# Sums of squares over heads: one plain float32 product, or two float32r products of squares that GpSimd splits

## The chip, the core and the metric

The kernel runs on one core of one Trainium2 chip. A core has a matrix engine, TensorE (PE in the profile; PEld is its loading of stationary operands), a vector engine, VectorE (DVE), a scalar engine, ScalarE (ACT), and GpSimd (POOL); SyncE (SP) issues transfers. Each engine works through its own queue in order, and the engines wait for each other by semaphores. The metric is the device time of one execution in microseconds; lower is better.

## What is computed

A two-layer model over 512 tokens of width 1024, all in float32. Layer 0 mixes tokens with stick-breaking attention and with a gated recurrence of 4 heads (`hgrn2`), layer 1 with sliding-window attention of 16 query heads and 4 key heads of width 64. Each layer then has a gated feed-forward part and a gated embedding. The part that matters here is the normalisation over the width of a head:

```python
def rmsnorm(x, g):
    xf = x.astype(jnp.float32)
    y = xf * lax.rsqrt(jnp.mean(xf * xf, axis=-1, keepdims=True) + EPS)
    return (y * g.astype(jnp.float32)).astype(x.dtype)
...
    o_b = rmsnorm(o_b.astype(h.dtype), hg_norm) * jax.nn.silu(gb.reshape(B, S, HG_HEADS, HG_DV))
...
    q = rmsnorm(q.reshape(B, S, SW_HEADS, SW_DIM), q_norm)
    k = rmsnorm(k.reshape(B, S, SW_KV_HEADS, SW_DIM), k_norm)
```

The first is taken over 4 heads of width 128 (layer 0), the other two over 16 and 4 heads of width 64 (layer 1).

## The kernel before

Activations lie feature by token: a tile has 128 features in its partitions and the 512 tokens along its rows. A large product is computed from split operands: weights and activations are each stored as a high and a low part in float32r, and three float32r products (high by high, high by low, low by high: lines 185 to 187, `mm3`) stand for one float32 product. Where no split was made, the kernel issues one plain float32 product.

A sum over the features of a head runs across partitions, so it is a product with a constant matrix. In `hg_head` (layer 0, run for each of the 4 heads) the head's output `pso` is squared by ScalarE (line 509, `osq`), a plain float32 product with a matrix of ones sums it (line 511, `pn`), ScalarE takes the logarithm and the exponential of the sum (`act`, line 71), and VectorE multiplies (line 515, `ob`). In `mixer_c` (layer 1) `project` squares each tile of two heads (line 729, `sqc`), and `normed` sums it by a plain product with a matrix that holds two blocks of ones (line 735, `pn`). That happens ten times: for two tiles of keys, and for eight tiles of queries, of which the first two come together and the other six one by one in the loop over `jt`, two rounds ahead of their use. So there are 14 such sums.

Around the four sums of layer 0 TensorE has the products of the stick-breaking attention's values (line 593, `poa`), the dense products (`psfm`) and the score products of the next head (`psd`, `psl`). Around the ten of layer 1 it has dense products, the products `pstm` of the values, and the attention's `pl`, `pt` and `poc`. `sp` is the pool of the statistics; its tag `sq` has two buffers.

The order on each engine is made by a scheduler when the program is built: it walks through the code's operations with its own estimate of their lengths and picks what it takes to be ready. The program that comes out has a fixed order on each engine. GpSimd has little to do before the change: constants at the start, small memsets, a few transfers.

Of the kernel before, what the change touches and what calls it, by code (L numbers as in the profile page):

```python
# [9 lines left out]
F32 = mybir.dt.float32  # L10
F32R = mybir.dt.float32r
U8 = mybir.dt.uint8
AF = mybir.ActivationFunctionType
ALU = mybir.AluOpType

P = 128
T = 512
# [8 lines left out]
SET_EL = "natural_log_exp_and_others"  # L26
# [24 lines left out]
class Kern:  # L51
# [34 lines left out]
    def bank(self, name, tag="mm"):  # L86

        if self.turn is None:
            return self.ps.tile([P, T], F32, tag=tag, name=name)
        i = self.turn % 8  # L90
        self.turn += 1
        if i % 2:
            return self.ps.tile([P, T], F32, tag="hg" if i % 4 == 3 else "mm", name=name)
        if i % 4 == 0:
            self.pair = self.zpair(name)
        return self.pair[:, i % 4 // 2, :]

    def setup(self):
        nc, A = self.nc, self.A
        self.cp = self.pool("const")  # L100
        self.hp = self.pool("hpool")
        self.xa = self.pool("xa", 16)
        self.wp = self.pool("wpool", 7)
        self.sp = self.pool("stat", 1)
        self.ps = self.pool("psum", 2, psum=True)
        self.turn = None
        cp = self.cp

        self.gains = cp.tile([P, V_CONV + 48], F32, name="gains")[:, 0:V_CONV]
        nc.scalar.dma_start(out=self.gains, in_=A["vecs"][:, 0:V_CONV])  # L110
        self.h = [self.hp.tile([P, T], F32, name=f"h{m}") for m in range(KT)]
        self.early = []
        for m in range(KT):
            nc.sync.dma_start(out=self.h[m], in_=A["xT"][m * P:(m + 1) * P, :])
            if m in EARLY:
                raw = self.wp.tile([P, 1024], F32, tag="wraw", name="wraw", bufs=2)
                for c in (slice(0, 512), slice(512, 1024)):
                    nc.sync.dma_start(out=raw[:, c], in_=A["w_ab"][EARLY[m]][:, c])
                self.early.append(raw)
        self.vec = cp.tile([P, NV - V_CONV], F32, name="vec")  # L120
        nc.gpsimd.dma_start(out=self.vec, in_=A["vecs"][:, V_CONV:])
        self.ones = cp.tile([P, P], F32, name="ones")
        nc.vector.memset(self.ones, 1.0)

        warm = self.bank("warm", "hg")
        for _ in range(WARM):
            nc.tensor.matmul(warm[:, 0:P], self.ones, self.ones, start=True, stop=True)
        self.eps = cp.tile([P, 1], F32, name="eps")
        nc.vector.memset(self.eps, EPS)
        self.rcol = cp.tile([P, NT], F32, name="rcol")  # L130
        self.one = cp.tile([P, 1], F32, name="one")
        nc.vector.memset(self.one, 1.0)
        self.cst = cp.tile([P, 3 * P], F32, name="cst")
        nc.gpsimd.dma_start(out=self.cst, in_=A["cst"][:, 0:3 * P])
        self.ident = self.cst[:, 0:P]
        self.flip = self.cst[:, P:2 * P]
        self.flips = self.cst[:, 0:2 * P]
        self.blk = self.cst[:, 2 * P:3 * P]
        self.cstr = cp.tile([P, 4 * P], F32R, name="cstr")
        self.ntri = self.cstr[:, 0:P]  # L140
        self.nones = self.cstr[:, P:2 * P]
        self.negm = self.cstr[:, 2 * P:3 * P]
        self.identr = self.cstr[:, 3 * P:4 * P]

    def matrices(self, tmp):
        nc = self.nc
        nc.gpsimd.dma_start(out=tmp[:, :3 * P], in_=self.A["cst"][:, 3 * P:6 * P])
        nc.gpsimd.tensor_copy(out=self.cstr[:, 0:3 * P], in_=tmp[:, 0:3 * P])
        nc.gpsimd.tensor_copy(out=self.cstr[:, 3 * P:4 * P], in_=self.ident)

    def v(self, c):
        if c < V_CONV:
# [86 lines left out]
    def square(self, m, st):  # L239
        nc = self.nc  # L240
        h = self.h[m]
        if m == 0:
            st["acc"] = self.sp.tile([P, T], F32, tag="acc", name="acc")
            nc.scalar.activation(st["acc"], h, AF.Square)
            return
        sq = self.sp.tile([P, T], F32, tag="sq", name="sq", bufs=2)
        nc.scalar.activation(sq, h, AF.Square)
        nc.vector.tensor_tensor(out=st["acc"], in0=st["acc"], in1=sq, op=ALU.add)
        if m == KT - 1:
            st["ss"] = [self.sp.tile([P, T], F32R, tag="sq", name=n, bufs=2) for n in ("sqhi", "sqlo")]  # L250
            nc.scalar.copy(out=st["ss"][0], in_=st["acc"])
            nc.vector.tensor_tensor(out=st["ss"][1], in0=st["acc"], in1=st["ss"][0], op=ALU.subtract)

    def norm(self, st, tag="mm"):

        nc = self.nc
        ps = self.bank("psn", tag)
        for i in range(2):
            nc.tensor.matmul(ps, self.nones, st["ss"][i], start=(i == 0), stop=(i == 1))
        r = self.sp.tile([P, T], F32, tag="rstd", name="rstd")  # L260
        self.act(SET_EL, r, ps, AF.Ln, scale=-1.0 / DM, bias=self.eps)
        self.act(SET_EL, r, r, AF.Exp, scale=-0.5)
        st["rstd"] = r
# [30 lines left out]
    def mixer_ab(self, st):  # L294
        nc, A = self.nc, self.A
        W = A["w_ab"]
        with ExitStack() as ctx:
# [3 lines left out]
            cp = self.pool("ab_const", 1, ctx=ctx)  # L301
# [89 lines left out]
            def hg_head(hd, q, k, p64):  # L391
# [11 lines left out]
                for b in range(NT):  # L403
# [3 lines left out]
                                        in1=self.flips.unsqueeze(1).broadcast_to([P, 2, 2 * P]), op=ALU.mult)  # L407

                ps = None
                for li in range(7):  # L410
# [8 lines left out]
                    n = T // (2 * c)  # L419
# [29 lines left out]
                    else:  # L449
                        for r in range(2):  # L450
                            h = slice(r * 64, r * 64 + 64)
                            nc.scalar.copy(out=ad.rearrange("p (j r) t -> p j r t", j=2)[h, :, r, 64:128],
                                           in_=po.rearrange("p (j r t) -> p j r t", j=2, r=2)[h, :, r, :])
# [47 lines left out]
                for j in range(NT):  # L501
                    nc.tensor.matmul(ps[:, j * P:(j + 1) * P], ib[j][:, vs], ad[:, j, :], start=first, stop=False, skip_group_check=True)
                    first = False
                    if j in off:
                        o = off[j]
                        nc.tensor.matmul(ps[:, (j + 1) * P:T], ib[j][:, vs], ao[:, o[0] * P:(o[-1] + 1) * P],
                                         start=False, stop=False, skip_group_check=True)
                sq = tp.tile([P, T], F32, tag="fp", name="osq", bufs=2)
                nc.scalar.activation(sq, ps, AF.Square)
                pn = bank("hg", "pn")  # L510
                nc.tensor.matmul(pn, self.ones, sq, start=True, stop=True)
                self.act(SET_EL, sq, pn, AF.Ln, scale=1.0 / P, bias=self.eps)
                self.act(SET_EL, sq, sq, AF.Exp, scale=-0.5)
                o = kp.tile([P, T], F32, tag="ob", name="ob")
                nc.vector.scalar_tensor_tensor(out=o, in0=ps, scalar=self.v(V_HGN), in1=sq, op0=ALU.mult, op1=ALU.mult)
# [123 lines left out]
            for i in range(4):  # L639
                d = dense(i + 1)  # L640
                h, s = hg_head(i, *heads[i]), sb_pair(i, *pairs[i])
                for c in PLAN if i < 3 else LAST:
                    next({"h": h, "s": s, "d": d}[c], None)
                for _ in d:
                    pass
# [55 lines left out]
    def mixer_c(self, st, bias, fill):  # L701
        nc, A = self.nc, self.A
        xs = st["xs"]
        W = A["w_c"]
        with ExitStack() as ctx:
# [26 lines left out]
            def normed(y, sq, gain, tag, bufs):  # L732

                pn = self.bank("pn")
                nc.tensor.matmul(pn, self.blk, sq, start=True, stop=True)  # L735
                self.act(SET_EL, sq, pn, AF.Ln, scale=1.0 / 64, bias=self.eps)
                self.act(SET_EL, sq, sq, AF.Exp, scale=-0.5)
                o = kp.tile([P, T], F32, tag=tag, name=tag, bufs=bufs)
                nc.vector.scalar_tensor_tensor(out=o, in0=y, scalar=gain, in1=sq, op0=ALU.mult, op1=ALU.mult)
                return o  # L740

            kn = [project(8 + i) for i in range(2)]
            kn = [normed(*x, self.v(V_KN), "kn", 2) for x in kn]
            vt = []
            for _ in tok:
# [78 lines left out]
            for jt in range(2):  # L824
                qs[jt] = normed(*two[jt], gq, "qn", 3)
            for jt in range(8):
                for n0 in (0, 2):
                    pend.append(scores(jt, n0))
                    if jt + 2 < 8:
                        if n0 == 0:  # L830
                            nxt = project(jt + 2)
                        else:
                            qs[jt + 2] = normed(*nxt, gq, "qn", 3)
                    if len(pend) > 2:
                        values(*pend.pop(0))
# [217 lines left out]
```

## Time and profile before

| | |
|---|---|
| time, median of 3 runs | 1327.49 us (1326.45 to 1328.64) |
| the profiled execution, its time | 1326.3 us |
| the profiled execution, its span | 1324.5 us |
| PE busy | 1309.1 us, 99% of the span |
| DVE busy | 863.1 us, 65% |
| ACT busy | 684.0 us, 52% |
| POOL busy | 18.7 us, 1% |
| granted clock of TensorE, mean | 0.999 |

The time holds the span of the profiled instructions and 1.8 us around it. In a row of the timeline the first number is the start in microseconds from the span's start, the second the duration; then come engine, line, operation, output and inputs, and shape; a row merges neighbours of one form and gives their count, and ends with the idle time before it and what ended that. A plain float32 product stands in the trace as two instructions, a float32r product as one. Ends of matrix products are modelled, so the start-to-start distance tells more than a duration.

### The profile page before, as it was taken

To read this page: it belongs to the slowest core of one execution; us is meant where nothing else is said; L and a number is where in the kernel's file an instruction comes from. 1 tells how busy PE (TensorE), PEld (TensorE's weight loads), DVE (VectorE), ACT (ScalarE), POOL (GpSimd) and SP (SyncE) were. 2 spreads that over 40 slices of the span, in tenths; PEclk is the share of its full clock that TensorE was granted. 3 is DMA by queue.
4 is the path that set the end of the run, shared out by engine and by line. 5 is a ranking of instruction groups with operands and counts; after the bars stand their busy time and mean duration, and the time that the engine had idled before them with its cause. 6 is when DMAs were issued, how large, how long until landed. Compare 5 with 4: busy or idle time off the path is not lost.

```text
span 1324.5 us, 16856 instructions
## 1 busy us (share of the span) xinstructions
PE 1309.1 (99%) x6162; PEld 1055.2 (80%) x6162; DVE 863.1 (65%) x1609; ACT 684.0 (52%) x1224; POOL 18.7 (1%) x108
## 2 busy tenths in 40 slices
PE   9999999999999999999999999999999999999998
PEld 7787767788888888888888866678888888888887
DVE  6567876766677347776558387755777536776555
ACT  6566876845345224444465466654544324455341
POOL 2000000000000000000000000000000000000000
PEclk9999999999999999999999999999999999999999
DMA  6321211134553333323333211122332333332332
GB/s 208 108 64 49 59 39 47 48 98 116 90 142 98 106 102 101 99 91 94 107 112 91 85 48 32 33 82 94 102 102 89 94 107 96 96 96 88 90 109 80
DMA packets 38821, 118.96 MB, mean 90 GB/s; under 512 B 4433, under 2 KB 10881, under 8 KB 38737
## 3 DMA queue, kind: packets, MB, share of 16 engines
q1 hardware_dynamic: 38032, 116.41, 29.5%
q0 software_dynamic: 560, 1.45, 0.5%
q8 instruction: 48, 0.79, 0.2%
q14 instruction: 37, 0.30, 0.1%
q10 hardware_dynamic: 144, 0.02, 0.0%
HBM read 115.37 MB, written 2.49 MB: 89 GB/s over the span
## 4 chain that ended last, share of the span: by engine, by line
PE 93%; DVE 4%; ACT 2%; issue 1%; DMA 0%; SPq 0%; DVEq 0%; ACTq 0%
PE psfm L185 25%; PE psfm L187 25%; PE psfm L186 25%; PE pl L765 2%; PE poc L817 2%; PE pstm L220 1%; PE pstm L218 1%; PE pstm L219 1%; PE pt L800 1%; PE poa L593 1%; ACT sl L71 1%; PE psz L576 1%; PE pn L735 1%; PE psl L443 1%; PE pspp L185 1%; PE pspp L187 1%
## 5 line engine op out<-in xcount | busy, mean ns | idle before, releaser
L185 PE MATMUL psfm<-xhi,whi 128*128 128x512 f32 (+1 forms) x1200 | 470.8, 393 | 1.3 <-ACT xhi L235 1.3
L170 ACT CAST whi<-wraw 128x512 fp32r<-128x512 f32 (+1 forms) x428 | 260.0, 613 | 406.2 <-PE psfm L186 319.9
L186 PE MATMUL psfm<-xlo,whi 128*128 128x512 f32 (+1 forms) x1200 | 467.0, 389 | 0.8 <-DVE xlo L236 0.7
L187 PE MATMUL psfm<-xhi,wlo 128*128 128x512 f32 (+1 forms) x1200 | 467.5, 390 | 0.1
L171 DVE TENSOR_TENSOR wlo<-wraw,whi 128x512 fp32r<-128x512 f32 (+1 forms) x428 | 287.9, 677 | 170.4 <-ACT whi L170 149.5
L185 PEld LDWEIGHTS psfm<-xhi,whi 128*128 128x128 f32 x1200 | 226.0, 188 | 49.3 <-issue 2.0
L186 PEld LDWEIGHTS psfm<-xlo,whi 128*128 128x128 f32 x1200 | 225.8, 188 | 48.8 <-DVE xlo L236 2.3
L187 PEld LDWEIGHTS psfm<-xhi,wlo 128*128 128x128 f32 x1200 | 225.5, 188 | 47.6 <-issue 1.3
L185 PE MATMUL psfm<-ghi,whi 128*128 128x512 f32 x352 | 136.9, 389 | 0.0
L186 PE MATMUL psfm<-glo,whi 128*128 128x512 f32 x352 | 136.9, 389 | 0.0
L187 PE MATMUL psfm<-ghi,wlo 128*128 128x512 f32 x352 | 136.9, 389 | 0.0
L858 DVE TENSOR_TENSOR u<-psfm,rstd 128x512 f32<-128x512 f32 x88 | 60.7, 691 | 64.0 <-PE psfm L187 60.4
L861 ACT ACTIVATE cy<-u,vec 128x512 f32<-128x512 f32 x88 | 71.7, 817 | 43.8 <-DVE u L858 43.8
L862 DVE SCALAR_TENSOR_TENSOR cy<-u,vec,cy 128x512 f32<-128x512 f32 x88 | 66.1, 752 | 39.0 <-ACT cy L861 38.9
L185 PEld LDWEIGHTS psfm<-ghi,whi 128*128 128x128 f32 x352 | 66.1, 188 | 13.7
L187 PEld LDWEIGHTS psfm<-ghi,wlo 128*128 128x128 f32 x352 | 66.1, 188 | 13.7
L186 PEld LDWEIGHTS psfm<-glo,whi 128*128 128x128 f32 x352 | 66.1, 188 | 13.7
L291 DVE TENSOR_TENSOR h<-h,psfm 128x512 f32<-128x512 f32 x48 | 33.0, 688 | 57.3 <-PE psfm L187 57.3
L863 DVE SCALAR_TENSOR_TENSOR cy<-u,vec,cy 128x512 f32<-128x512 f32 x88 | 65.9, 751 | 2.7
L875 ACT CAST ghi<-cy 128x512 fp32r<-128x512 f32 x44 | 27.4, 623 | 49.4 <-DVE cy L872 49.4
L236 DVE SCALAR_TENSOR_TENSOR xlo<-h,gains,xhi 128x512 fp32r<-128x512 f32 x48 | 36.5, 761 | 7.0 <-ACT xhi L235 6.6
L235 ACT ACTIVATE xhi<-h,gains 128x512 fp32r<-128x512 f32 x48 | 34.6, 724 | 11.0 <-DVE h L291 6.8
(216 smaller groups left out, 1303.3 us busy)
## 6 DMA issues: line engine op xcount, KB each, us to landing
wraw<-w_up SPq DMA_DIRECT2D x88, 512.0 KB, 3.5
wraw<-w_dn SPq DMA_DIRECT2D x32, 512.0 KB, 3.5
wraw<-w_ab SPq DMA_DIRECT2D x18, 512.0 KB, 3.5
wraw<-w_pg SPq DMA_DIRECT2D x16, 512.0 KB, 3.5
wraw<-w_dn SPq DMA_DIRECT2D x32, 192.0 KB, 2.3
wraw<-w_c SPq DMA_DIRECT2D x10, 512.0 KB, 3.4
wraw<-w_abo SPq DMA_DIRECT2D x8, 512.0 KB, 3.6
wraw<-w_co SPq DMA_DIRECT2D x8, 512.0 KB, 3.5
```

The lines of the kernel that those rows point to most:

```text
L170: nc.scalar.copy(out=hi[:, :d1 - d0], in_=r)
L171: nc.vector.tensor_tensor(out=lo[:, :d1 - d0], in0=r, in1=hi[:, :d1 - d0], op=ALU.subtract)
L185: t.matmul(ps, w[0], x[0], start=first, stop=False)
L186: t.matmul(ps, w[0], x[1], start=False, stop=False)
L187: t.matmul(ps, w[1], x[0], start=False, stop=last)
L235: nc.scalar.activation(hi, h, AF.Identity, scale=g)
L236: nc.vector.scalar_tensor_tensor(out=lo, in0=h, scalar=g, in1=hi, op0=ALU.mult, op1=ALU.subtract)
L291: self.nc.vector.tensor_tensor(out=self.h[m], in0=self.h[m], in1=ps, op=ALU.add)
L858: nc.vector.tensor_tensor(out=u[:, 2:], in0=ps, in1=rstd, op=ALU.mult)
L861: nc.scalar.activation(y, u[:, 2:], AF.Identity, scale=w[2], bias=w[3])
L862: nc.vector.scalar_tensor_tensor(out=y, in0=u[:, 1:T + 1], scalar=w[1], in1=y, op0=ALU.mult, op1=ALU.add)
L863: nc.vector.scalar_tensor_tensor(out=y, in0=u[:, 0:T], scalar=w[0], in1=y, op0=ALU.mult, op1=ALU.add)
```

## The change

A new helper `sums` splits the squares on GpSimd into a high part (a cast to float32r) and a low part (square minus high part), and sums them by two float32r products into the same bank. Both sites call it. The matrix of ones of layer 0 becomes the existing `nones`, which holds minus ones, so the sign of the scale turns; the block matrix `blk` moves to the constants that are stored as float32r, and the transfers and casts of the constants are cut differently (256 and 512 columns, before 384 and 384).

```diff
-        self.cst = cp.tile([P, 3 * P], F32, name="cst")
-        nc.gpsimd.dma_start(out=self.cst, in_=A["cst"][:, 0:3 * P])
+        self.cst = cp.tile([P, 2 * P], F32, name="cst")
+        nc.gpsimd.dma_start(out=self.cst, in_=A["cst"][:, 0:2 * P])
...
-        self.blk = self.cst[:, 2 * P:3 * P]
-        self.cstr = cp.tile([P, 4 * P], F32R, name="cstr")
...
+        self.cstr = cp.tile([P, 5 * P], F32R, name="cstr")
+        self.blk = self.cstr[:, 0:P]
...
-        nc.gpsimd.dma_start(out=tmp[:, :3 * P], in_=self.A["cst"][:, 3 * P:6 * P])
-        nc.gpsimd.tensor_copy(out=self.cstr[:, 0:3 * P], in_=tmp[:, 0:3 * P])
-        nc.gpsimd.tensor_copy(out=self.cstr[:, 3 * P:4 * P], in_=self.ident)
+        nc.gpsimd.dma_start(out=tmp, in_=self.A["cst"][:, 2 * P:6 * P])
+        nc.gpsimd.tensor_copy(out=self.cstr[:, 0:4 * P], in_=tmp)
+        nc.gpsimd.tensor_copy(out=self.cstr[:, 4 * P:5 * P], in_=self.ident)
...
+    def sums(self, pn, by, sq):
+
+        nc = self.nc
+        ss = [self.sp.tile([P, T], F32R, tag="sq", name=n, bufs=2) for n in ("sqhi", "sqlo")]
+        nc.gpsimd.tensor_copy(out=ss[0], in_=sq)
+        nc.gpsimd.tensor_tensor(out=ss[1], in0=sq, in1=ss[0], op=ALU.subtract)
+        for i in range(2):
+            nc.tensor.matmul(pn, by, ss[i], start=(i == 0), stop=(i == 1))
...
-                nc.tensor.matmul(pn, self.ones, sq, start=True, stop=True)
-                self.act(SET_EL, sq, pn, AF.Ln, scale=1.0 / P, bias=self.eps)
+                self.sums(pn, self.nones, sq)
+                self.act(SET_EL, sq, pn, AF.Ln, scale=-1.0 / P, bias=self.eps)
...
-                nc.tensor.matmul(pn, self.blk, sq, start=True, stop=True)
+                self.sums(pn, self.blk, sq)
```

Nine lines are added ahead of `norm`, so a line behind them has a number that is 9 higher in the changed kernel.

On GpSimd the queue after the constants (`cstr`, `hgm`) changes as follows, first before, then now; `u` is a tile of the feed-forward part:

```order
L149 CAST cstr<-cst 128x128
L148 CAST cstr<-cstt 128x384
L312 CAST hgm<-mf 128x3x128 x4
L857 MEMSET u 128x2 x2
L674 DMA bias<-relb 32x16
```

```order
L149 CAST cstr<-cst 128x128
L148 CAST cstr<-cstt 128x512
L321 CAST hgm<-mf 128x3x128 x4
L258 CAST sqhi<-osq 128x512
L259 ISA
L259 TENSOR_TENSOR sqlo<-osq,sqhi 128x512
L258 CAST sqhi<-osq 128x512
L259 TENSOR_TENSOR sqlo<-osq,sqhi 128x512
```

A cast and a subtraction for each of the four heads now stand between the constants and the memsets (ten more pairs stand in layer 1), and ahead of the first subtraction the program has an instruction `ISA` that it names a reload of GpSimd's library.

On TensorE, the end of the second head of layer 0, where `pso` is that head's output; the third head is alike, before and then now:

```order
L502 MATMUL pso<-ad,ib 128x128
L593 MATMUL poa<-sl,va 64x128 x2
L593 MATMUL poa<-sl,va 64x256
L511 MATMUL pn<-osq,ones 128x512
L593 MATMUL poa<-sl,va 64x256
L593 MATMUL poa<-sl,va 64x384 x2
L593 MATMUL poa<-sl,va 64x512 x2
L405 MATMUL psd<-qh,kk 128x128
```

```order
L511 MATMUL pso<-ad,ib 128x128
L602 MATMUL poa<-sl,va 64x128 x2
L602 MATMUL poa<-sl,va 64x256 x2
L602 MATMUL poa<-sl,va 64x384
L261 MATMUL pn<-sqhi,cstr 128x512
L602 MATMUL poa<-sl,va 64x384
L602 MATMUL poa<-sl,va 64x512
L261 MATMUL pn<-sqlo,cstr 128x512
L602 MATMUL poa<-sl,va 64x512
```

The first product of the sum moved behind two more value products, the second stands two value products later, and the score product `psd` comes after four dense products. In the first head the second product stands much further back: 18 dense products and a block of score products `psz` lie between the last value product and it, and `psd` comes after it.

On TensorE, where the first two query tiles of layer 1 are normalised, before and then now:

```order
L187 MATMUL psfm<-xhi,wlo 128x512
L735 MATMUL pn<-sqc,cst 128x512 x2
L185 MATMUL psfm<-xhi,whi 128x512
L186 MATMUL psfm<-xlo,whi 128x512
L187 MATMUL psfm<-xhi,wlo 128x512
```

```order
L187 MATMUL psfm<-xhi,wlo 128x512
L261 MATMUL pn<-sqhi,cstr 128x512
L261 MATMUL pn<-sqlo,cstr 128x512
L261 MATMUL pn<-sqhi,cstr 128x512
L185 MATMUL psfm<-xhi,whi 128x512
L186 MATMUL psfm<-xlo,whi 128x512
L261 MATMUL pn<-sqlo,cstr 128x512
L774 MATMUL pl<-kn,qn 128x128 x2
```

Between the second tile's two products stand two dense ones. On ScalarE the logarithm of the first tile's sum now stands ahead of the second tile's square, where it stood behind it. At the other sums the two products stand as follows: fourth head of layer 0, high part behind two dense products and one more of them between; key tiles, the four products of the two tiles spread among 256-column products `pstm`, four ahead of the first and then three, two and three between them; third query tile, high part behind all of `pl`, one dense product between; the next three query tiles, high part ahead of the last three `poc`, low part behind them; the last two, both where the plain product stood.

## Rows read from the trace of the kernel before

**Rows 1.** The page, busy time, share and instructions of each engine.

```profile
PE 1309.1 (99%) x6162; PEld 1055.2 (80%) x6162; DVE 863.1 (65%) x1609; ACT 684.0 (52%) x1224; POOL 18.7 (1%) x108
```

**Rows 2.** Timeline of PE in dense float32r products, first and last of a run of 30.

```profile
900.09 0.39 PE L186 MATMUL psfm<-xlo,whi 128*128 128x512 f32 x1
...
906.66 0.39 PE L185 MATMUL psfm<-xhi,whi 128*128 128x512 f32 x1
```

**Rows 3.** Timeline around the sums of the two key tiles, PE and ACT.

```profile
736.54 1.17 ACT L729 ACTIVATE sqc<-y 128x512 f32<-128x512 f32 x2 [0.82 <-DVE y L727]
...
737.79 1.96 PE L735 MATMUL pn<-sqc,cst 128*128 128x512 f32 x4
...
739.83 0.29 PE L220 MATMUL pstm<-whi,xlo 128*128 128x256 f32 x1
...
741.02 0.28 PE L218 MATMUL pstm<-whi,xhi 128*128 128x256 f32 x1
```

**Rows 4.** Timeline of POOL at the start.

```profile
7.13 0.29 POOL L149 CAST cstr<-cst 128x128 fp32r<-128x128 f32 x1 [3.07 <-DMA cst<-cst]
8.00 0.51 POOL L148 CAST cstr<-cstt 128x384 fp32r<-128x384 f32 x1 [0.57 <-DMA cstt<-cst]
9.17 3.57 POOL L312 CAST hgm<-mf 128x384 uint8<-128x384 f32 x4 [0.66 <-DMA mf<-hgm]
```

**Rows 5.** One line's instructions (minimum, median, maximum ns; first and last start).

```profile
L248 DVE TENSOR_TENSOR acc<-acc,sq x42: 677/684/991, 9.6 to 1277.3; 128x512 f32<-128x512 f32 x42
```

**Rows 6.** Transfers by line: count, KB each, median us from issue to landing.

```profile
mf<-hgm POOLq DMA_DIRECT2D x2, 192.0 KB, 6.2
```

**Rows 7.** Timeline at the end of layer 0's second head, PE and ACT.

```profile
167.25 0.60 ACT L509 ACTIVATE osq<-pso 128x512 f32<-128x512 f32 x1 [1.16 <-PE pso L502]
167.94 1.12 PE L511 MATMUL pn<-osq,ones 128*128 128x512 f32 x2
169.00 2.15 PE L593 MATMUL poa<-sl,va 128*64 128x256 f32 x10
...
171.08 0.49 PE L405 MATMUL psd<-qh,kk 128*128 128x128 f32 x2
```

**Rows 8.** Timeline at the end of layer 0's fourth head, PE and ACT.

```profile
254.87 0.60 ACT L509 ACTIVATE osq<-pso 128x512 f32<-128x512 f32 x1
...
255.60 1.05 PE L511 MATMUL pn<-osq,ones 128*128 128x512 f32 x2
...
257.20 0.39 PE L186 MATMUL psfm<-xlo,whi 128*128 128x512 f32 x1
```

**Rows 9.** Timeline around the sums of the first two query tiles, PE and ACT.

```profile
751.74 0.63 ACT L729 ACTIVATE sqc<-y 128x512 f32<-128x512 f32 x1 [0.33 <-DVE y L727]
...
756.25 1.02 PE L735 MATMUL pn<-sqc,cst 128*128 128x512 f32 x2
...
757.77 0.67 ACT L71 ACTIVATE sqc<-pn,eps 128x512 f32<-128x512 f32 x1
757.92 1.12 PE L735 MATMUL pn<-sqc,cst 128*128 128x512 f32 x2 [0.65 <-ACT sqc L729]
...
759.35 0.40 PE L187 MATMUL psfm<-xhi,wlo 128*128 128x512 f32 x1
```

**Rows 10.** Timeline at the third query tile's sum, PE.

```profile
767.93 1.12 PE L735 MATMUL pn<-sqc,cst 128*128 128x512 f32 x2 [0.61 <-ACT sqc L729]
...
769.95 0.39 PE L186 MATMUL psfm<-xlo,whi 128*128 128x512 f32 x1
```

**Rows 11.** Timeline at the last query tile's sum, PE and ACT.

```profile
833.88 0.64 ACT L729 ACTIVATE sqc<-y 128x512 f32<-128x512 f32 x1
...
836.39 1.12 PE L735 MATMUL pn<-sqc,cst 128*128 128x512 f32 x2
...
837.36 1.04 PE L800 MATMUL pt<-cst,lg 128*128 128x128 f32 x8
```

**Rows 12.** Who waited for whom, window of layer 0's heads (us in total, times, longest).

```profile
PE psl L443 <- DVE ad L445: 5.2, 3, 1.7
```

More of the change, by code (lines that the diff above doesn't have):

```diff
@@ L137, in setup @@
         self.flips = self.cst[:, 0:2 * P]
-        self.blk = self.cst[:, 2 * P:3 * P]
-        self.cstr = cp.tile([P, 4 * P], F32R, name="cstr")
[L140 to L143, printed above, removed]
+        self.cstr = cp.tile([P, 5 * P], F32R, name="cstr")
+        self.blk = self.cstr[:, 0:P]
+        self.ntri = self.cstr[:, P:2 * P]
+        self.nones = self.cstr[:, 2 * P:3 * P]
+        self.negm = self.cstr[:, 3 * P:4 * P]
+        self.identr = self.cstr[:, 4 * P:5 * P]
     def matrices(self, tmp):
         nc = self.nc
-        nc.gpsimd.dma_start(out=tmp[:, :3 * P], in_=self.A["cst"][:, 3 * P:6 * P])
-        nc.gpsimd.tensor_copy(out=self.cstr[:, 0:3 * P], in_=tmp[:, 0:3 * P])
-        nc.gpsimd.tensor_copy(out=self.cstr[:, 3 * P:4 * P], in_=self.ident)
+        nc.gpsimd.dma_start(out=tmp, in_=self.A["cst"][:, 2 * P:6 * P])
+        nc.gpsimd.tensor_copy(out=self.cstr[:, 0:4 * P], in_=tmp)
+        nc.gpsimd.tensor_copy(out=self.cstr[:, 4 * P:5 * P], in_=self.ident)
     def v(self, c):
```

## The prediction, made before the changed kernel ran

> **What bounds the kernel now.** I first read the busy shares: TensorE is busy for 1309.1 of 1324.5 us, VectorE 65%, ScalarE 52%, GpSimd 1% [rows 1]. So a microsecond that TensorE is spared is worth up to a microsecond, and one that it stands still costs one; there are only 15.4 us of idle time to win. Then I read the timelines at the 14 sums for two things: how far TensorE's next start is moved by a sum, and how long the square had been ready when TensorE came to it. For the second the reader looks for the end of the square on ScalarE and the start of `pn` on TensorE: where the two lie 0.1 us apart, as in layer 0 [rows 7], any later delivery shows up in the time; where `pn` starts 1.9 us after the square [rows 11], there is cover.
>
> **What the change takes away.** Thirty dense float32r products start (906.66 - 900.09)/29 = 0.227 us apart [rows 2]. The plain float32 pair of the key tiles starts at 737.79; the products behind it are (741.02 - 739.83)/10 = 0.119 us apart, and the third of them starts at 739.83, so the pair took 739.83 - 0.24 - 737.79 = 1.80 us, 0.90 each [rows 3]. Two float32r products cost 0.45 instead of 0.90, and 14 sums save 14 x 0.45 = 6.3 us of TensorE's time. That is all that the change can give directly.
>
> **What it adds.** Each square now passes through two GpSimd instructions before TensorE can finish the sum. The cast: 128 columns took 0.29 us and 384 took 0.51 [rows 4], so 0.86 ns a column and 0.18 us fixed, 0.62 us for 512. The subtraction reads two operands, and no such instruction of GpSimd is in this trace. Its lower bound is the cast's 0.62 us. For the upper bound I take the slowest cast there is: four of 384 columns took 3.57 us beside VectorE's work, 0.89 each [rows 4], less 0.18 fixed 1.85 ns a column, and for two operands of 512 columns 0.18 + 1024 x 0.00185 = 2.07 us. I take 1.24 us, two plain casts, since the plain cast to the same type is the nearest row; 0.62 and 2.07 stay as ends. A handover costs about 0.1 us (square ends 167.85, `pn` starts 167.94 [rows 7]). So the high part can be multiplied 0.1 + 0.62 + 0.1 = 0.82 us after the square, the low part 0.82 + 1.24 + 0.1 = 2.16 us after it. [...]
>
> **The sum, site by site**, against the work that TensorE had done at the same point before. S is the end of the square.
>
> Second and third head of layer 0 [rows 7]: S = 167.85. The value products `poa` come in pairs that fill half the array each and overlap: ten instructions with 2048 columns took 169.00 to 171.08, 1.02 ns a column. TensorE, which came to the plain product at 167.94, now has 640 more columns ahead of the sum, 0.65 us, to 168.59; the high part is ready at 168.67 and done at 168.90; 896 columns follow, with their broken pair about 1.1 us, to 170.0; the low part is ready at 170.01, done 170.24; the last 512 columns, alone, 0.91: 171.15 against 171.08. Cost 0.1 each: the saving is eaten by one more broken pair and the wait.
>
> First head, in the same clock: high part done 168.90, all 1408 columns behind it (1.6 us) to 170.5 instead of 171.08, the low part 0.23 later: -0.3. Its low part waits for the library reload, whose price no row shows: at least nothing, at most about the slowest transfer that GpSimd issues, 6.2 us [rows 6]. The low part is ready at 170.0 plus the reload, and TensorE comes to it after 18 dense products, 170.5 + 4.1 = 174.6, and a score block that I don't count: 4.6 us or more are hidden, so the reload costs 0 to 1.6 us; I take 0. [...]
>
> Fourth head [rows 8]: S = 255.47. Two dense products more, then a wait for the high part until 256.29; one dense product; the low part is ready at 257.63, done 257.86, against 257.20 before: +0.7.
>
> Key tiles [rows 3]: the two squares end at 737.71 (736.54 + 1.17) and, one square of 0.63 us behind the start, at 737.17. Four 256-column products, high part to 738.50, three more to 738.86, then a wait for the low part until 739.33. GpSimd takes the second cast only now (739.33 to 739.95): its high part at 740.05, its low part at 741.39, done 741.62, against 741.02: +0.6.
>
> First two query tiles [rows 9]: the first square ended at 752.37, so its parts are there when TensorE comes at 756.25; both are done at 756.70. ScalarE's logarithm of it, 0.67 us, now stands ahead of the second square: that one ends at 757.47 + 0.63 = 758.10. Its high part follows at 758.92, two dense products to 759.60, its low part at 760.26, done 760.49, against 759.35: +1.1. Here TensorE stands still about 2.9 us, for 0.65 before, and nothing else is queued ahead that could fill it.
>
> Third query tile [rows 10]: S = 767.88; high part 768.70, one dense product, low part 770.04, done 770.27, against 769.95: +0.3.
>
> Last five query tiles, one shown [rows 11]: S = 834.52, the plain product started at 836.39 and held TensorE for 0.97 us. The low part is ready at 836.68, the high part's product (with the switch from one kind of product to the other about 0.3) is done then, and the next product starts at 836.96 instead of 837.36: -0.4. In three of the five the parts stand apart and pay one switch more: -0.35 on average, -1.75 for the five.
>
> The larger transfer of constants (512 columns for 384) and its longer cast, 0.11 us, lie in the first 9 us, long before a sum of squares is taken: nothing. GpSimd's memsets and transfers behind the splits start later than 258 us and wait for others anyway: nothing.
>
> Sum: -0.3 + 2 x 0.1 + 0.7 + 0.6 + 1.1 + 0.3 - 1.75 = **+0.9 us**. Of the 6.3 us saved nearly all goes into waiting. Against the profiled execution that is 1326.3 + 0.9 = 1327.2; the median of the runs lies 1.2 us above that execution, so 1328.4 us on the scale of medians.
>
> **How far it can move.** With a subtraction of 0.62 us the waits shrink at six sites, and the same walk gives -2.4 us. With 2.07 us it gives about +10: each sum but the first then waits, two of them twice, because the second tile's cast stands behind the first tile's subtraction.
>
> **The rivals.** *All waits hidden*: TensorE gains the full 6.3 us, 1321.2 us. For it speaks that the order was made so that the products come when their parts are due by the scheduler's estimate; against it that the gaps left for a subtraction are often one to three products, 0.2 to 0.7 us, less than even a cast takes. It also needs the stall of 5.2 us in three places at the score products [rows 12] to go away or stay as it is.
>
> *GpSimd is held up beside VectorE*: slower, 1337.5 us at the upper end. During the four casts at 9.2 to 12.7 us VectorE's additions took up to 0.99 us, for a median of 0.68 [rows 4, 5]: each slowed the other. A weight split of VectorE falls beside nearly every split of squares in layer 1. It decides from a subtraction (with its waiting) of about 1.4 us on: each 0.1 us more costs about 1 us over all sites, and 0.9 + 1.8 us is what can be measured.
> [...]
>
> *The reload or the late start of the next head*: a reload above 6 us, or the first head's `psd` five microseconds later than before, so that score products wait for VectorE more than the 5.2 us of now [rows 12]: 3 to 6 us, about 1332.5.
>
> *The products are not cheaper* can be left at 2%: float32r products of this very kind cost 0.227 us [rows 2].
>
> **How the numbers follow.** Forecast (waits eat the gain): 0.45. All or most waits hidden: 0.18. GpSimd held up: 0.22. Reload or next head: 0.13. The rest 0.02. A measurement of this kernel can tell about 0.2%, 2.7 us. Of the forecast 0.41 lies within that, 0.03 above and 0.01 below; both slow cases (0.35) lie above; of the fast case 0.17 lies below and 0.01 within; the rest is halved between same and slower. That makes 0.18 faster, 0.43 same, 0.39 slower. The range reaches from 1322.5, which leaves most of the full gain out, to 1337, near the upper end of the held-up GpSimd.
>
> **What would show it.** TensorE's idle time in the window of the heads and in layer 1's attention up by about 6 us in all, with "GpSimd `sqlo`" as what ended it; two float32r `pn` products at 0.2 to 0.3 us each; a subtraction near 1.24 us; the largest new waits at the first two query tiles (about 2.9 us) and at the key tiles. Wrong would make it a subtraction under 0.7 us or over 1.6 us, a stall of several microseconds at the first low part, or new waits at `psl`.

## The result, and where the time went

The changed kernel takes **1336.1 us** (six runs, 1334.5 to 1337.4) against 1327.3 (six runs, 1326.5 to 1328.6): a ratio of 1.0065, 95% interval 1.0054 to 1.0075, so 8.8 us **slower**. That lies within the range, but not in the forecast, which was no measurable change. The profiled execution has a span of 1334.8 us, 10.3 above that of before. The page of after, to be held against [rows 1], and TensorE's longest waits by tile:

```profile
PE 1310.8 (98%) x6162; PEld 1057.8 (79%) x6162; DVE 864.5 (65%) x1609; ACT 682.6 (51%) x1224; POOL 47.7 (4%) x136
```

```profile
PE psl L452 <- DVE ad L454: 5.2, 4, 1.7
PE pn L261 <- POOL sqhi L258: 3.8, 4, 2.1
PE pn L261 <- POOL sqlo L259: 3.3, 6, 0.9
PE psl L452 <- ACT l L71: 2.2, 2, 1.6
PE psfm L185 <- ACT xhi L235: 1.8, 1, 1.8
```

(Line numbers behind 253 are nine higher than before; L258 is the cast, L259 the subtraction, L261 the product.) TensorE was to be busy 6.3 us less and is busy 1.7 us *more*: its products became cheaper and something else in its busy time dearer. Its idle time went from 15.4 to 24.0 us. Where, is read by cutting both timelines at four instructions that every version has: the first `pstm` product (about 22 us), VectorE's first `u` of layer 0's feed-forward (about 318), the first `pstm` of layer 1's attention, the first `u` of layer 1's feed-forward. All versions run here, cut in the same way (one profiled execution each; the medians stand beside). One execution of q1plain and one of direct ran in a slower state, and the ratios leave them out.

| us | start | layer 0's heads | between | attention | rest | median of runs |
|---|---|---|---|---|---|---|
| before | 21.85 | 295.53 | 413.40 | 197.64 | 396.08 | 1327.3 |
| **after** | 23.43 | 300.26 | 413.40 | 201.66 | 396.05 | 1336.1 |
| const | 23.15 | 295.55 | 413.41 | 197.56 | 396.03 | 1327.4 |
| heads | 23.31 | 300.35 | 413.37 | 197.59 | 396.08 | 1331.8 |
| attn | 21.17 | 295.48 | 413.45 | 201.46 | 396.04 | 1330.9 |
| tail | 22.02 | 295.50 | 413.40 | 201.25 | 396.03 | 1328.7 |
| q1plain | 23.10 | 300.23 | 413.38 | 200.61 | 396.08 | 1335.1 |
| fill | 22.20 | 300.45 | 413.38 | 197.33 | 396.04 | 1330.9 |
| nolow | 23.78 | 294.22 | 413.41 | 189.98 | 396.11 | 1318.5 |
| idle | 21.41 | 295.50 | 413.43 | 198.30 | 396.06 | 1327.9 |
| vsplit | 22.23 | 299.85 | 413.40 | 201.96 | 396.06 | 1335.7 |
| direct | 22.16 | 292.98 | 413.40 | 189.11 | 396.05 | 1316.4 |
| mix3 | 21.94 | 295.51 | 413.44 | 196.66 | 396.05 | 1325.0 |
| mix2 | 21.83 | 295.56 | 413.38 | 196.54 | 396.09 | 1326.2 |

The heads lost 4.73 us and the attention 4.02, together 8.75, close to the 8.8 of the medians. The 1.6 us of the start are not the change's: with the same constants the start takes 21.2 to 23.8 us.

**GpSimd's instructions are as long as forecast.** Minimum, median and maximum of one instruction in ns, and the first split in time:

```profile
L258 POOL CAST sqhi<-sqc x10: 609/660/1129, 743.5 to 846.0; 128x512 fp32r<-128x512 f32 x10
L259 POOL TENSOR_TENSOR sqlo<-sqc,sqhi x10: 1262/1282/1631, 744.2 to 847.2; 128x512 fp32r<-128x512 f32 x10
```

```profile
123.77 0.61 POOL L258 CAST sqhi<-osq 128x512 fp32r<-128x512 f32 x1 [111.07 <-ACT osq L518]
124.47 1.27 POOL L259 TENSOR_TENSOR sqlo<-osq,sqhi 128x512 fp32r<-128x512 f32 x1
```

Forecast were 0.62 and 1.24 us. The first subtraction of the program starts 0.09 us behind its cast: no cost of a reload is to be seen. Three instructions that ran beside VectorE's were longer, and TensorE waited for the low parts behind them:

```profile
261.38 1.59 POOL L259 TENSOR_TENSOR sqlo<-osq,sqhi 128x512 fp32r<-128x512 f32 x1
745.60 0.95 POOL L258 CAST sqhi<-sqc 128x512 fp32r<-128x512 f32 x1
766.29 1.63 POOL L259 TENSOR_TENSOR sqlo<-sqc,sqhi 128x512 fp32r<-128x512 f32 x1
```

Against 1.27 and 0.61 us these are 0.32, 0.34 and 0.36 us more, some 1.0 us of the 8.8.

**Heads.** TensorE at the second head's sum, against [rows 7] and the start of the block before (first row):

```profile
167.15 0.86 PE L593 MATMUL poa<-sl,va 128*64 128x128 f32 x6
...
168.73 1.51 PE L602 MATMUL poa<-sl,va 128*64 128x128 f32 x10
170.53 0.50 PE L261 MATMUL pn<-sqhi,cstr 128*128 128x512 f32 x1 [0.29 <-POOL sqhi L258]
170.97 1.08 PE L602 MATMUL poa<-sl,va 128*64 128x384 f32 x4
171.97 0.49 PE L261 MATMUL pn<-sqlo,cstr 128*128 128x512 f32 x1
172.40 1.07 PE L602 MATMUL poa<-sl,va 128*64 128x512 f32 x2
173.40 0.50 PE L185 MATMUL psfm<-xhi,whi 128*128 128x512 f32 x1
...
185.30 0.68 PE L452 MATMUL psl<-e 128*128 128x128 f32 x4 [0.85 <-DVE ad L454]
```

From the first value product to the end of the block it is 173.40 - 168.73 = 4.67 us; before, 171.08 - 167.15 = 3.93. Between half-width value products a full product takes 0.43 us, not 0.23 (170.53 to 170.97): the two take 0.86 us, the plain one 1.06 (167.94 to 169.00), so a sum saves only 0.2 us here. The wait for the high part adds 0.3. The rest, the 16 value products themselves, takes 3.5 us instead of 2.9: the sum now breaks their pairs in two places instead of one. The last 512 columns, left alone, take 1.00 us (172.40 to 173.40), where 2048 columns took 2.08 before [rows 7]. Then a score product of the next head waits 0.85 us for VectorE; its counterpart before didn't wait. The third head repeats it (+0.43 and 0.85); the fourth lost 1.1 at its sum (a wait of 0.94 for `sqlo`, 0.32 of it by the longer subtraction above); the first gained 0.2. All waits at `psl` grew from 5.8 to 7.9 us. Some 0.5 us of the 4.73 I can't place.

**Attention.** TensorE at the first two query tiles, against [rows 9], and its granted clock there (stretch, length, busy time of PE, PEld, DVE, ACT, POOL, then the clock):

```profile
763.56 0.39 PE L261 MATMUL pn<-sqhi,cstr 128*128 128x512 f32 x1
763.79 0.39 PE L261 MATMUL pn<-sqlo,cstr 128*128 128x512 f32 x1
766.26 0.50 PE L261 MATMUL pn<-sqhi,cstr 128*128 128x512 f32 x1 [2.09 <-POOL sqhi L258]
...
767.97 0.79 PE L261 MATMUL pn<-sqlo,cstr 128*128 128x512 f32 x1 [0.75 <-POOL sqlo L259]
768.69 1.66 PE L774 MATMUL pl<-kn,qn 64*128 64x128 f32 x8
770.28 0.79 PE L187 MATMUL psfm<-xhi,wlo 128*128 128x512 f32 x1
770.87 0.63 PE L185 MATMUL psfm<-xhi,whi 128*128 128x512 f32 x1
771.30 0.63 PE L186 MATMUL psfm<-xlo,whi 128*128 128x512 f32 x1
```

```profile
766.00:768.00 2.00, 0.99 (x4) 0.52 (x4) 0.75 (x1) 0.00 (x0) 1.84 (x2) 0.96 0.00 0
768.00:774.00 6.00, 6.00 (x18) 4.14 (x19) 2.43 (x11) 1.32 (x2) 0.00 (x0) 0.50 0.01 3
774.00:776.00 2.00, 2.00 (x9) 1.59 (x8) 0.69 (x1) 1.48 (x6) 0.00 (x0) 0.83 0.00 0
```

TensorE stands still 2.09 + 0.75 us, as forecast. What was not: behind it the granted clock is 0.50 from 767.9 to 774.7 us, and dense products start 0.43 us apart instead of 0.227. That costs half of 6.8, 3.4 us, and shows as busy time. Before, the same stretch had 1.00. The other executions agree: the mean granted clock is 0.993 to 0.996 in the six of the changed kernel, and 0.996 to 0.999 in those of the kernel before. The last query tile, against [rows 11], is the gain that was meant:

```profile
834.29 0.50 PE L261 MATMUL pn<-sqhi,cstr 128*128 128x512 f32 x1
834.63 0.42 PE L261 MATMUL pn<-sqlo,cstr 128*128 128x512 f32 x1
834.88 1.04 PE L809 MATMUL pt<-cst,lg 128*128 128x128 f32 x8
```

0.59 us instead of 0.97. From the first to the last transpose `pt`, five sums, after needs 89.92 us, before 91.61.

### The profile page after: what moved, and what is told of

Read it like the earlier page. It is cut to its first block, busy times and chain, and to the rows that moved or that the text cites. A ratio compares the mean times of both kernels' runs of the same rounds, so it can differ in the third digit from the quotient of the medians.

```text
span 1334.8 us, 16936 instructions
## 1 busy us (share of the span) xinstructions
PE 1310.8 (98%) x6162; PEld 1057.8 (79%) x6162; DVE 864.5 (65%) x1609; ACT 682.6 (51%) x1224; POOL 47.7 (4%) x136
## 4 chain that ended last, share of the span: by engine, by line
PE 89%; DVE 5%; ACT 3%; issue 1%; POOL 1%; DMA 1%; SPq 0%; POOLq 0%; ACTq 0%; DVEq 0%
PE psfm L185 25%; PE psfm L186 25%; PE psfm L187 25%; PE poc L826 1%; PE pstm L219 1%; PE pstm L220 1%; PE pstm L218 1%; PE pl L774 1%; ACT sl L71 1%; PE pt L809 1%; PE poa L602 1%; PE pn L261 1%; POOL sqlo L259 1%; DVE ad L454 1%; PE pspp L187 1%
```

## The experiments

**Theory:** the low part comes 2.2 us behind the square, TensorE meets that at the tight places, the broken pairs and the later next head add to it in layer 0, and in the attention a pause makes its clock fall. **Rivals:** the rearranged constants at the start; GpSimd and VectorE holding each other up; the clock falling for another reason than the pause.

### Only the constants (const)

In this part a line with + or - is one against the changed kernel, for heads and idle against the kernel before; `...` marks what is left out.

```diff
-                self.sums(pn, self.nones, sq)
...
+                nc.tensor.matmul(pn, self.ones, sq, start=True, stop=True)
...
+            nc.gpsimd.dma_start(out=blkf, in_=A["cst"][:, 2 * P:3 * P])
...
-                self.sums(pn, self.blk, sq)
+                nc.tensor.matmul(pn, blkf, sq, start=True, stop=True)
```

> Constants laid out and loaded at the start as in the changed kernel, but all 14 sums stay plain float32 products (the block matrix for layer 1 is loaded a second time, as float32, late, by one more GpSimd transfer). In the trace of the changed kernel 1.6 us were already lost at 122 us, before the first sum, where TensorE's granted clock stood at its lower level until 16.8 us instead of 13.6. If the rearranged constants do that: 1328.9 us and the low clock up to about 16.8 us. If it varies from execution to execution, or comes from something else in the change: 1327.3.

1327.4 us, ratio 1.0001 (0.9992 to 1.0010). The constants cost nothing, the start varies from execution to execution.

### One layer alone (heads, attn)

```diff
-                nc.tensor.matmul(pn, self.ones, sq, start=True, stop=True)
...
+                self.sums(pn, self.nones, sq)
...
```

This is heads; attn has the reverse in layer 0 of the changed kernel.

> Only the four sums of layer 0's heads are split, constants as before. Theory (delivery by GpSimd, broken pairs of value products, a later next head): between the first and the end of the fourth head the changed kernel lost 3.9 us, so 1331.2 us. Rival (the loss is all behind the query tiles' stall and its clock): 1327.3 to 1328. My prediction's own terms gave +0.6 here: 1327.9.

> Only the ten sums of layer 1's attention are split, layer 0's heads are plain; constants as in the changed kernel. Theory: key tiles +1, second query tile's stall and the lower clock behind it +4.3, last five -1.6, together +4 to +4.5, so 1331.5 us, and 1333 if the start's 1.6 us comes with the constants. My prediction's own terms gave +0.25: 1327.6. Rival (GpSimd held up beside VectorE everywhere): also the last five lose, above 1334.

1331.8 us (1.0036, 1.0023 to 1.0049) and 1330.9 (1.0027, 1.0016 to 1.0038): by these ratios +4.8 and +3.6, together 8.4 of the 8.8. Each loses in its own stretch of the table alone.

### Only the last five query tiles (tail)

```diff
...
+                            qs[jt + 2] = normed(*nxt, gq, "qn", 3, jt + 2 > 2)
```

The last argument says whether this sum is split; the heads, the key tiles and the first three query tiles stay plain.

> Only the sums of the last five query tiles are split, all others plain; constants as in the changed kernel. There the square lies 1.9 us or more ahead of TensorE. Theory: each gains 0.35 us, 1327.3 - 1.7 = 1325.6 us (1327.2 if the start's 1.6 us comes with the constants). Rival (GpSimd's work slows VectorE and with it the rest): 1328 or more.

1328.7 us, ratio 1.0011 (1.0002 to 1.0019): a miss. The order was made anew, with the low product of the first split far behind and the value products `poc` beside the sums, where they now wait for VectorE's copies. TensorE in this kernel:

```profile
794.06 0.44 PE L831 MATMUL poc<-wt,vt 128*64 128x128 f32 x4 [0.98 <-DVE wt L823]
794.43 0.50 PE L261 MATMUL pn<-sqlo,cstr 128*128 128x512 f32 x1
794.87 1.01 PE L831 MATMUL poc<-wt,vt 128*64 128x128 f32 x6
795.80 1.97 PE L814 MATMUL pt<-cst,lg 128*128 128x128 f32 x8
...
810.48 0.44 PE L831 MATMUL poc<-wt,vt 128*64 128x128 f32 x4 [1.09 <-DVE wt L823]
```

```profile
795.00:800.00 5.00, 5.00 (x28) 3.43 (x29) 3.15 (x11) 3.51 (x10) 0.00 (x0) 0.66 0.00 0
```

Eight transposes take 1.97 us at the lower clock, 1.04 above. Behind the second of these pauses the mean clock is 0.71 from 810 to 815 us. So pauses of 0.98 and 1.09 us among short products were followed by falls as well. The profiled execution lost 3.6 us in the attention, the median of the runs 1.2: six executions with a mean granted clock of 0.997 took 1327.4 to 1328.7 us, five with 0.994 to 0.996, the profiled one among them, 1329.6 to 1331.7. That fits a clock that doesn't fall alike in all executions of one program; why, is open.

### Is it the pause that makes the clock fall? (q1plain, fill)

In q1plain the second query tile's sum alone is plain again; in fill the third projection is written between the first and the second tile's sum.

```diff
+            qs[0] = normed(*two[0], gq, "qn", 3)
+            nxt = project(2)
+            qs[1] = normed(*two[1], gq, "qn", 3)
...
```

> The changed kernel with one sum, that of the second query tile, plain again; the other 13 stay split. In the changed kernel TensorE paused 2.1 and 0.75 us there, and from 767.9 to 774.6 us its granted clock was 0.50. Theory (the clock fell because of the pause): the sum's 1.1 us and the 3.3 us of the low clock both go, 1336.1 - 4.4 = 1331.7 us, and the clock stays 1.00 there. Rival (only the pause itself costs, the clock has another cause): 1335.0 us, the clock still falls.

> The changed kernel, all 14 sums split, but the projection of the third query tile (24 dense products, 5.4 us) is written ahead of the second query tile's sum, so that TensorE has work while GpSimd splits that square. Theory: the second tile's pause of 2.84 us and the low clock behind it go; the third tile's sum now follows its own projection closely and waits up to 1.1 us for its low part. About 1332 us if the clock stays at 1.00 behind that shorter wait; 1334 or more if the clock falls there instead. Rival (the pause alone, no part of the clock): 1335.

q1plain: 1335.1 us. The theory's number was missed by 3.4 us and the rival's, 1335.0, came out; but the trace gives another reason than the rival's: the pause has moved to the third query tile, and the fall with it.

```profile
775.77 0.49 PE L261 MATMUL pn<-sqhi,cstr 128*128 128x512 f32 x1 [1.27 <-POOL sqhi L258]
777.13 0.61 PE L261 MATMUL pn<-sqlo,cstr 128*128 128x512 f32 x1 [0.86 <-POOL sqlo L259]
```

```profile
763.00:770.00 7.00, 5.64 (x27) 3.61 (x26) 4.31 (x13) 3.66 (x6) 0.00 (x0) 1.00 0.22 74
777.00:784.00 7.00, 6.87 (x15) 4.81 (x16) 4.06 (x19) 3.58 (x12) 0.07 (x1) 0.53 0.08 33
```

At the old place a pause of 1.36 us is left and the clock is 1.00; the fall lasts from 777.4 to 784.2 us. So the fall moved with the two pauses and doesn't belong to the place. And three executions took 1334.5 to 1335.2 us at a mean granted clock of 0.995 or 0.996, the fourth 1330.8 at 0.998. That is near the theory's number, and such a mean leaves at most 3.3 us lost to the clock, the start's included, so this execution can't have had the whole of that fall.

fill: 1330.9 us, 5.2 below the changed kernel, with all 14 sums split. Its pauses there are 0.37 and 1.19 us, and the fall is shorter, 3.4 us:

```profile
775.00:780.00 5.00, 5.00 (x17) 4.03 (x16) 4.06 (x24) 5.00 (x24) 0.00 (x0) 0.67 0.00 0
```

The attention takes 197.33 us with it, 0.3 less than before the change: with the long pause the loss of that stretch is gone. The time lies below both of the theory's numbers, though the clock did fall.

### Without the low part (nolow)

```diff
...
-        nc.gpsimd.tensor_tensor(out=ss[1], in0=sq, in1=ss[0], op=ALU.subtract)
-        for i in range(2):
-            nc.tensor.matmul(pn, by, ss[i], start=(i == 0), stop=(i == 1))
+        nc.tensor.matmul(pn, by, ss[0], start=True, stop=True)
```

> The changed kernel without the low part: no subtraction and no second product at any of the 14 sums, so the rounding remainder of the squares is left out of the sums. Theory: 14 x 0.23 = 3.2 us of products, some 3.3 us of waits for low parts and one broken pair in each of three heads (1.2 us) go; the pause of 2.1 us for the second query tile's high part stays and the clock falls behind it: about 1328.4 us. If the clock does not fall: 1325. Rival (the cast alone is what delays TensorE, the subtraction is hidden): 1332.

1318.5 us, 17.6 below the changed kernel: more than twice the 7.7 that my sum gave, and more than its 11.1 without a fall, with 6.0 us in the heads and 11.7 in the attention. The low part costs that with all that hangs on it. A pause of 2 us for the high part is left, and the clock stays at 1.00 behind it:

```profile
758.05 0.50 PE L259 MATMUL pn<-sqhi,cstr 128*128 128x512 f32 x1 [2.04 <-POOL sqhi L258]
```

```profile
755.00:765.00 10.00, 7.96 (x38) 5.57 (x36) 5.41 (x17) 6.11 (x17) 0.62 (x1) 1.00 0.20 59
```

So a long pause doesn't always bring a fall. Two close to each other don't either: these are those of the changed kernel's third query tile, and from 776 to 790 us its clock is 1.00.

```profile
780.50 0.50 PE L261 MATMUL pn<-sqhi,cstr 128*128 128x512 f32 x1 [1.17 <-POOL sqhi L258]
781.86 0.50 PE L261 MATMUL pn<-sqlo,cstr 128*128 128x512 f32 x1 [0.63 <-POOL sqlo L259]
```

In attn TensorE pauses 2.09 us until 759.33 and 0.62 us until 761.03, and the clock is low from the start of this stretch, before the second pause begins:

```profile
760.00:761.00 1.00, 0.41 (x2) 0.00 (x0) 0.00 (x0) 0.00 (x0) 0.98 (x1) 0.51 0.00 0
```

Each fall in these traces, those of the start and the last few us aside, stands behind a pause of about 1 us or more (0.98 in tail the shortest). Which pauses bring one, the runs don't show: behind the waits of up to 1.74 us at `psl` the clock stays at 1.00, from 60 to 320 us before and after the change.

### GpSimd's work without a reader (idle)

```diff
+                nc.gpsimd.tensor_copy(out=ds[0], in_=sq)
+                nc.gpsimd.tensor_tensor(out=ds[1], in0=sq, in1=ds[0], op=ALU.subtract)
...
```

> The kernel before, all sums plain, but GpSimd also splits the ten squares of layer 1's attention (same cast, same subtraction), and nobody reads the parts. Contention alone: 1327.5 us if GpSimd's work beside VectorE costs the kernel nothing, 1329 or more if it holds VectorE up where TensorE waits for it.

1327.9 us, ratio 1.0006 (0.9997 to 1.0015): no loss that can be measured, 0.7 us in the table. So the ten splits of layer 1 don't hold VectorE up where TensorE waits for it. The four of the heads aren't in this run; there vsplit, below, has the same waits of 0.8 us at `psl` without GpSimd, and nearly the same loss (299.85 for 300.26). Nor can this run show what it costs that GpSimd is held up, since nobody waits for its parts: that is the 1.0 us read above. The contention is there in both directions: GpSimd's three instructions above were 0.32 to 0.36 us longer beside VectorE's. The other way, VectorE and GpSimd in the changed kernel, one instruction each, from their timelines:

```profile
744.57 1.51 DVE L171 TENSOR_TENSOR wlo<-wraw,whi 128x512 fp32r<-128x512 f32 x1
```

```profile
744.24 1.28 POOL L259 TENSOR_TENSOR sqlo<-sqc,sqhi 128x512 fp32r<-128x512 f32 x1
```

VectorE's subtraction, begun 0.33 us into GpSimd's, took 1.51 us for the usual 0.68: it ended 0.56 us behind GpSimd's.

### The split on other engines (vsplit)

```diff
-        nc.gpsimd.tensor_copy(out=ss[0], in_=sq)
-        nc.gpsimd.tensor_tensor(out=ss[1], in0=sq, in1=ss[0], op=ALU.subtract)
+        nc.scalar.copy(out=ss[0], in_=sq)
+        nc.vector.tensor_tensor(out=ss[1], in0=sq, in1=ss[0], op=ALU.subtract)
```

> The changed kernel with the split made by ScalarE (cast, 0.61 us a 512-column tile) and VectorE (subtraction, 0.68) instead of GpSimd; all 14 sums split, products the same. Theory (the low part comes too late, 2.16 us behind the square): the low part would come about 1.6 us behind the square where both engines are free, so the pauses shrink by up to 0.6 us at the tight places and the key and query tiles lose less: about 1333 us. Rival (the queues of the two busier engines take more than GpSimd's slowness): 1337 or more.

1335.7 us, as slow as with GpSimd: inconclusive by its number, told apart by its trace. The key tiles' stretch (first `pstm` to first query projection) drops to 13.75 us, for 14.56 before and 15.53 with GpSimd; the last five tiles need 100.11 us for 91.61. There TensorE waits for ScalarE, whose copies are now queued beside the casts, and behind two of these pauses, of 1.29 us each (of four such), its clock falls to 0.50 for 3.4 us a time, which makes 3.4 of the 8.5 us lost:

```profile
PE pn L261 <- ACT sqhi L258: 5.4, 7, 2.3
PE poc L826 <- ACT wt L818: 5.2, 4, 1.3
```

Shorter latency helped at the key tiles, where the square is late; at the last five, where it is early, GpSimd's free queue was the better place (89.92 us for 100.11).

### One product, no handover (direct)

```diff
...
+        self.nc.tensor.matmul(pn, by, sq, start=True, stop=True)
...
+                sq = tp.tile([P, T], F32R, tag="sqc", name="sqc")
...
```

> ScalarE writes each square straight as float32r and TensorE multiplies it once; no GpSimd instruction and no low part, so the rounding remainder of the squares is left out of the sums. Theory (the products are 0.67 us cheaper each and only the handover eats it): 14 x 0.67 = 9.4 us below the kernel before, 1317.8 us; with the cast on GpSimd in the way the same sums took 1318.5, so 1317 to 1318. Rival (a gain of TensorE is lost at other waits, as VectorE's at the score products): 1321 or more.

1316.4 us, ratio 0.9914 (0.9901 to 0.9928), 10.7 below the kernel before for 9.4 forecast. The products are at least as cheap as computed, and no other wait takes their place.

### Versions meant to beat both (mix3, mix2)

```diff
+        nc.gpsimd.tensor_tensor(out=self.dum, in0=self.eps, in1=self.one, op=ALU.subtract)
...
+                qs[jt] = normed(*two[jt], gq, "qn", 3, jt == 0)
...
+                            qs[jt + 2] = normed(*nxt, gq, "qn", 3, jt > 0)
```

This is mix3; mix2 also has the moved projection of fill.

> A version meant to beat both at full precision: split only the first query tile and the last five, whose squares are early; the four heads, both key tiles and the second and third query tile stay plain. GpSimd also makes one subtraction of a single column at the start, so that the low products are not placed late in the order, as they were when only the last five were split (1328.7 us, two pauses of 1.0 and 1.1 us at the value products and the clock at 0.83 and 0.85 behind them). Theory: the low product stands next to the high one again, no pause, no fall of the clock, six sums gain 0.35 us each: 1327.2 - 2.1 = 1325.1 us. Rival (any use of the split costs what it saves): 1327 or more.

> As the last, but the third query tile's projection written ahead of the second query tile's sum, so that this sum can be split too, seven in all (only the third query tile, the key tiles and the heads plain). Theory: the second tile's pause goes as in the kernel with the moved projection, the third tile's plain sum waits less than 1 us, seven sums gain 0.35 us: 1327.2 - 2.5 = 1324.8 us if the clock holds at 1.00 in the whole of the attention. Rival (a pause of the order of 1 us at the value products, as in the kernel with only the last five split, and the clock falls): 1328 or more.

mix3: **1325.0 us**, ratio 0.9982 (0.9973 to 0.9991), faster than both at the same precision. That it came out at the 1325.1 forecast is in part luck. Its profiled execution gains 1.0 us in the attention, not 2.1: the last five sums still wait 0.32 to 0.54 us each for the low part. The rest goes along with the clock: ten of its eleven executions have a mean granted clock of 0.998 or 0.999, eighteen of the 21 of the kernel before beside them 0.996 or 0.997, and the three others of those took 1326.3 to 1326.6 us. Whether the change has a part in that isn't shown. From 745 to 865 us the clock of mix3 is 1.00 in every stretch of 10 us. mix2: 1326.2 us, 0.9991 (0.9982 to 1.0000): its own forecast of 1324.8 was missed by 1.4. Its attention takes 196.54 us for mix3's 196.66, but its executions spread from 1324.6 us at a mean clock of 0.999 to 1327.7 at 0.995. The profiled one, 1325.2, has pauses of 1.06 and 1.09 us at the value products, as tail had, without a fall behind them; the rival's fall may have come in others.

## Why the prediction was right or wrong

- **The saving** (0.45 us a sum): near it where the two products stand together, not among half-width ones. The last query tile shows 0.59 for 0.97, the second head's block 0.86 for 1.06, and direct gives back 0.76 us a sum at most (10.7 / 14), the 0.67 of one product less with something over.
- **Cast and subtraction** (0.62 and 1.24): right, 0.61 and 1.27, with three instructions 0.3 us longer beside VectorE.
- **The reload** (0 to 1.6 us, taken as 0): right, 0.09 us between cast and subtraction.
- **Heads:** the step that failed. Forecast +0.6, measured +4.73. The second and third head were put at +0.1 each: the block of the second head is +0.74. I took the full product between half-width ones at 0.23 us, it took 0.43, which makes 0.4 for the two; the wait for the high part was 0.3 instead of 0.1; the broken pair, 0.6, I had about right. The fourth was put at +0.7 and lost 1.1. And I let each head end at its own sum: the score products of the next heads wait 2.1 us more in all, which stood only in the rival on the late start of the next head.
- **Key tiles:** +0.6 forecast, +0.97 measured. **First two query tiles:** +1.1, measured +1.27, with the pause of 2.84 us for 2.9 forecast.
- **Third query tile:** the other step that failed. +0.3 forecast, +3.68 from the first score product to the first transpose, 3.4 of it by TensorE's lower clock behind the pause. I had priced every pause by its length.
- **Last five:** -1.75 forecast, -1.69 measured.
- **Rivals.** GpSimd held up beside VectorE named the right time (1337.5 at its end), for the most part for the wrong reason: its subtraction has a median of 1.28 us, not the 1.4 or more from which the rival was to decide, and the three longer instructions make some 1.0 us. VectorE's subtraction of 1.51 us beside GpSimd's shows that [rows 5], with 0.99 at most, gave too small a size of the contention. The late start of the next head, the rival at 1332.5, is what happened in layer 0. The sum went by a walk in which nearly all of the gain was eaten; with 4.1 us more in the heads and 3.4 for the clock it comes out at 8.4, for 8.8 measured. That the time lies in the range is in part luck: nothing in the sum or in a rival has the clock, and the upper end came from a rival that made 1.0 us.
- **What would show it:** idle time by 8.6 us more for the 6 forecast, ended more often by the high part than I had it (3.8 us for `sqhi`, 3.3 for `sqlo`); subtraction and the pause as said, products too outside the half-width runs; new waits at `psl`, which I had named as what would make me wrong, and which did.

## What to carry to other kernels

Splitting the operand bought a cheaper product (0.59 us for 0.97 at the last query tile) with a longer way to it (1.97 us from the start of the first cast to the end of its subtraction), so change only the sites where the operand is ready well before TensorE comes: here six of fourteen gave 1.0 us in the stretch that was changed (2.4 by the medians) and all fourteen lost 8.8. A pause of TensorE cost more than its length where the clock fell behind it (3.4 us on top of 2.84 at the second query tile); look at the granted clock after each new pause, and put independent dense work into it (5.2 us less in fill). And a product set into a run of half-width ones cost twice its dense price here, 0.43 us for 0.23, and broke a pair.

## What the runs showed of the hardware

- A fall of TensorE's granted clock from 1.00 to 0.50 behind pauses of 2.09 and 0.75 us and of 1.27 and 0.86 us, lasting 6.8 us, and falls of 3.4 us behind pauses of about 1 us in tail, fill and vsplit; none behind a single one of 2.04 us in nolow, nor behind 1.17 and 0.63 us in the changed kernel. The falls followed waits; a wait alone did not settle it.
- The low clock of the start (0.50) lasts 3.4 us in some executions and 6.8 in others and ends between 12.5 us (attn) and 17.3 (nolow); the start of nearly the same program takes 21.17 to 23.78 us.
- A VectorE subtraction beside one of GpSimd took 1.51 us instead of 0.68; subtractions of GpSimd beside VectorE took 1.59 and 1.63 us instead of 1.27.
